# HGRN heads advanced in pairs, and the value products of a query block issued in one visit

## The chip, the cores and the metric

One NeuronCore of a Trainium2 chip runs the whole kernel. The metric is device time in microseconds of one execution; the figure used is the median of several runs.

## What is computed

Two residual layers over 512 tokens of width 1024, in float32. Each layer normalises its input, projects it to 15 pieces, runs three token mixers beside each other and merges them:

```python
for l in range(DEPTH):                       # 2
    h = rms_norm(x, norm_gain[l])
    proj = jnp.einsum('bld,dn->bln', h, w_in[l])
    (qa, fa_f, fa_b, ia, za, ub, vb, zb, qc, kc, vc, zc, g_a, g_b, g_c) = split(proj)
    # A: bidirectional gated linear recurrence, 4 heads, dk = dv = 128
    ya = rms_norm(hgrn2_bidirectional(qa, fa_f, fa_b, ia, lower[l]), hg_norm_gain[l]) * silu(za)
    # B: chunked spatial gating
    yb = spatial_gating(gelu(ub), gelu(vb), ...) * silu(zb)
    # C: windowed attention, 8 query heads on 2 kv heads, rotary, per-head sink
    yc = window_attention(q, k, vc, sink_logits[l]) * silu(zc)
    merged = sigmoid(g_a) * (ya @ w_branch_a[l]) + sigmoid(g_b) * (yb @ w_branch_b[l]) \
           + sigmoid(g_c) * (yc @ w_branch_c[l])
    x = x + merged @ w_out[l]
```

## The kernel before

**Projections.** Every weight tile of 128 x 1024 is loaded on SP's queue in the order of `weight_plan` (line 46; the host packs them in that order), split into a high part by ScalarE (line 193) and a low part by VectorE (line 194), and used in three matmuls per 128 rows of contraction: `t_block` (line 424, matmuls at line 433) with the weights stationary and 512 tokens moving, `nat_block` (line 390, matmuls at line 386) with the tokens stationary. A block of `main_t` has 24 such matmuls. `w_next` and `w_ahead` keep the loads and splits some tiles ahead.

**Side work.** The rest of the layer is written as Python generators in the list `sides`: normalisation and rotation of queries and keys, one `attention(qb)` for each of four query blocks, one `gla(h)` for each HGRN head, `ln_v` and `spatial(g)`. `advance(us)` is called in the middle and at the end of each projection block. It adds to a credit and steps the first two generators of the list (WIDTH = 2) in turn; a step yields its cost, and a yield of None makes that generator wait for the next `advance`. `flush` runs generators to their end; it stands before each of the three merge loops (lines 1010 to 1015), for attention, for the spatial part, and for everything.

**What a head does.** `gla` (line 739) builds the intra-chunk scores by levels m = 1, 2, 4, ... 128. The sum product and levels 1 to 8 are 32 products of a 32-wide stationary each, all into slots of one PSUM tile `cb` (line 769); levels 16 and 32 stand at line 794, also 32-wide, level 64 at line 803, 64-wide, level 128 at line 818, 128-wide. Between the levels VectorE copies or merges slots into `pc` (lines 782, 787, 810) and multiplies the decays into q and k (line 827) and the gates (line 830), and ScalarE mixes k for the next level (line 758). Each level ends with a cost of 2.6 and a None. Then follow a transposition (line 842), the state (line 849), the output (lines 859, 866), its normalisation, and a transposition back (line 880).

**What attention does.** For each key block of a query block VectorE transposes the probabilities in 32 x 32 pieces (line 670), POOL's queue writes them to DRAM and reads them back rearranged (lines 672, 673), four Nones later two value products of a 64-wide stationary and 512 columns follow (line 680; four instruction records for a key block).

**Order.** The program text gives each instruction a priority; within it a scheduler places, on each engine, what is ready by its own timing model, and adds all waits. Only instructions wrapped in `pin` keep their order (the loads on SP among them). In the main loop (line 948) the blocks of a head come first, then `gla(h)` joins the list; the vb projection stands behind head 0, u and z blocks of the spatial branch behind heads 1 and 2.

Of the kernel before, what the change touches and what calls it, by code (L numbers as in the profile page):

```python
# [13 lines left out]
F32 = mybir.dt.float32  # L14
# [7 lines left out]
P = 128  # L22
# [23 lines left out]
def weight_plan():  # L46

    plan = []

    def nat(c):  # L50
        for i in range(4):
            plan.append(("n", c, i))

    nat(C_QC)
    for g in range(2):
        plan.append(("z", g))
    for i in range(2):
        plan.append(("k", C_KV, i))
    for g in range(2, 4):
        plan.append(("z", g))  # L60
    nat(C_IA)
    for h in range(H):
        for c in (C_QA, C_FF, C_FB, C_ZA):
            plan.append(("t", c + P * h))
        if h == 0:
            nat(C_VB)
        elif h < 3:
            for g in (2 * h - 2, 2 * h - 1):
                plan.append(("t", C_UB + P * g))
                plan.append(("t", C_ZB + P * g))  # L70
    for br, cg in ((2, C_GC), (1, C_GB), (0, C_GA)):
        for j in range(KT):
            plan.append(("t", cg + P * j))
            if j % 2 == 0:
                plan.append(("b", br, j))
    for u in range(2):
        for i in range(4):
            plan.append(("o", u, i))
    return plan
# [51 lines left out]


N_RAW, N_HI, N_LO = 4, 5, 4
STAGGER = 2
N_M4, N_T2, N_PM, N_PS = 22, 7, 3, 5


def build(nc, tc, cp, wp, sb, pp, dp, x, wpk, brow, gainb, pvec, wsp, trig, amask, imask, out):
    V, S, G, E = nc.vector, nc.scalar, nc.gpsimd, nc.tensor
# [4 lines left out]
    def nm(s):  # L144
        cnt[0] += 1
        return f"{s}_{cnt[0]}"

    def m4(shape=(P, 1024), dt=F32):
        return sb.tile(list(shape), dt, name=nm("m4"), tag="m4", bufs=N_M4)
# [10 lines left out]
    def ps_side(shape=(P, 512), dt=F32):  # L160
        return pp.tile(list(shape), dt, name=nm("ps"), tag="ps", bufs=N_PS)
# [276 lines left out]
    sides = []  # L438
# [21 lines left out]
    def advance(us):  # L460
# [6 lines left out]
            credit[0] -= c  # L467
        credit[0] = min(credit[0], 2.0 * us if sides else 0.0)

    def flush(upto=()):  # L470
        while sides and (not upto or any(u in sides for u in upto)):
            step([])
        credit[0] = min(credit[0], 0.0)
# [3 lines left out]
    for l in range(L):  # L477
# [63 lines left out]
        vC = t2((P, NT, P))  # L541
# [77 lines left out]
        def attention(qb):  # L619
            k0, k1 = max(qb - 1, 0), min(qb + 2, NT)  # L620
            while not (("q", qb) in done and ("k", (k1 - 1) // 2) in done):
                yield None
            for _ in range(STAGGER * (qb % 2)):
                yield None
            nkb = k1 - k0
            nk = nkb * P
            off = (k0 - qb + 1) * P
            rc, dn, mxs, m, esk = small(8), small(8), small(8), small(8), small(8)
            sms, pair, pts = [], [], {}
            for h in range(8):  # L630
                g = h // 4
                if h % 2 == 0:
                    sm2 = m4((P, 2, nk))
                    pair.append(sm2)
                sms.append(sm2[:, h % 2, :])
                sp = ps_side()
                E.matmul(sp[:, :nk], qt[qb][:, h, :], ktt[0][:, g, k0 * P : k1 * P], start=True, stop=False)  # L637
                E.matmul(sp[:, :nk], qt[qb][:, h, :], ktt[1][:, g, k0 * P : k1 * P], start=False, stop=True)  # L638
                V.tensor_tensor_reduce(
                    sms[h], sp[:, :nk], am[:, off : off + nk], 1.0, NEG, ALU.add, ALU.max, mxs[:, h : h + 1]  # L640
                )
                yield 0.5
                if h == 3:
                    yield None
            V.tensor_tensor(m, mxs, sink, ALU.max)
            V.tensor_tensor(esk, sink, m, ALU.subtract)
            V.tensor_scalar_mul(m, m, -1.0)
            for h in range(8):
                S.activation(sms[h], sms[h], AF.Exp, bias=m[:, h : h + 1], accum_out=dn[:, h : h + 1])
                if h == 3:  # L650
                    yield 0.0
                    yield None
            S.activation(esk, esk, AF.Exp)
            V.tensor_tensor(dn, dn, esk, ALU.add)
            V.reciprocal(rc, dn)
            yield 0.5
            yield None
            for h in range(8):
                V.tensor_scalar_mul(sms[h], sms[h], rc[:, h : h + 1])
            yield 2.0  # L660
            yield None

            po = ps_side((P, 4, 4, 32))
            for kb in range(nkb + 1):
                if kb < nkb:
                    pt = m4((P, 4, 256))
                    xb = pt.rearrange("p b (h j) -> p b h j", j=32)
                    for i in range(4):
                        src = pair[i][:, :, kb * P : (kb + 1) * P].rearrange("p h (b j) -> p h b j", j=32)
                        V.transpose(xb[:, :, 2 * i : 2 * i + 2, :].rearrange("p b h j -> p h b j"), src)  # L670
                    pd = dp.tile([P, 4, 256], F32, name=nm("pd"))
                    G.dma_start(pd, pt)
                    G.dma_start(pt, pd.rearrange("(a j) b n -> (j b) a n", j=32))
                    pts[kb] = pt
                    yield 1.0
                for _ in range(4):
                    yield None
                if kb > 0:
                    for g in range(2):
                        E.matmul(  # L680
                            po[64 * g : 64 * g + 64],
                            vC[:, k0 + kb - 1, 64 * g : 64 * g + 64],
                            pts[kb - 1][:, :, 128 * g : 128 * g + 128],
                            start=kb == 1,
                            stop=kb == nkb,
                            tile_position=(0, 64 * g),
                        )
                    yield 1.0
            yield None
            qs = slice(qb * P, (qb + 1) * P)  # L690
            for i in range(2):
                z = szc[i][:, :, qs].rearrange("p h (a t) -> p h a t", t=32)
                V.tensor_tensor(z, po[:, :, 2 * i : 2 * i + 2, :].rearrange("p a h t -> p h a t"), z, ALU.mult)
            yield 1.5
# [11 lines left out]
        for g in range(4):  # L706
# [6 lines left out]
            po = main_t()  # L713
            z = szc[g // 2][:, g % 2, :]
# [185 lines left out]
        def ln_v():  # L900
            mv = small(8)
            mv2 = mv.rearrange("p (n c) -> p n c", c=2)
            for n in range(NT):
                st = small(6)
                V.bn_stats(st, vg[n // 2][:, n % 2, :])
                V.bn_aggr(mv2[:, n, :], st)
            r = rstd(mv2[:, :, 1], NT, 1.0)

            po = ps_side((P, 4, P))
            E.matmul(po, ones, ws, start=True, stop=True)  # L910
            for g in range(4):
                b = br[:, g * P : (g + 1) * P]
                V.scalar_tensor_tensor(b, po[:, g, :], lnb[:, g : g + 1], b, ALU.mult, ALU.add)
            yield 2.5
            yield None
            for n in range(NT):
                v = vg[n // 2][:, n % 2, :]
                V.tensor_scalar(v, v, mv2[:, n, 0:1], r[:, n : n + 1], ALU.subtract, ALU.mult)
                yield 0.7
# [24 lines left out]
            advance(2.6)  # L944


        lnv, spat = ln_v(), [spatial(g) for g in range(4)]
        for h in range(H):
            po = main_t()
            q = t2()  # L950
            S.copy(q, po)
            advance(2.6)
            ff, kd = m4((P, 2, T)), m4((P, 2, T))
            for d in range(2):
                po = main_t()
                gates(po, d, h, ff, kd)
                advance(2.6)
            po = main_t()
            z = yA[h // 2][:, h % 2, :]
            S.activation(z, po, AF.Sigmoid)  # L960
            V.scalar_tensor_tensor(z, po, hg[:, h : h + 1], z, ALU.mult, ALU.mult)
            sides.append(gla(h, q, ff, kd, z))
            advance(2.6)
            if h == 0:
                nat_units(do_vb, 2.6)
                sides.insert(0, lnv)
                if more:
                    rr = rope_row(l + 1)
                    tabs[0] = rope_tables(rr)
            elif h < 3:  # L970
                do_uz(2 * h - 2)
                do_uz(2 * h - 1)
                if h == 2:
                    sides[1:1] = spat


        acc, mgh, mgl = [], [], []
# [158 lines left out]
```

## Time and profile before

| | |
|---|---|
| median of 3 runs | 1115.63 us (1115.42 to 1116.74) |
| the profiled execution | 1115.61 us, its span 1113.8 us |
| TensorE busy | 1102.2 us (99%) in 7012 matmul records |
| weight loads busy | 895.1 us (80%) |
| VectorE busy | 699.1 us (63%) |
| ScalarE busy | 428.4 us (38%) |
| granted TensorE clock | 0.998 of full speed |

The span runs from the first to the last instruction of the program. Matmuls overlap in the records: a projection matmul is shown 0.39 us long, while the next one starts 0.23 us after it. What TensorE really spends is therefore read from the starts, or from the chain of work that ended last, which cuts the overlaps.

### The profile page before, as it was taken

Reading aid. Unit: us, or ns where it says so; the run is one execution under the profiler, and the core shown is the slowest. Engines: PE = TensorE matmul, PEld = TensorE weight load, DVE = VectorE, ACT = ScalarE, POOL = GpSimd, SP = SyncE. Lnnn points to the kernel's source line nnn. Section 1 sums busy time; section 2 is a strip of 40 time slices with the busy share of each in tenths; the row PEclk is TensorE's granted clock in tenths of the full one; section 3 lists DMA queues with packets and bytes.
Section 4 is the critical chain, followed back from the end, with each engine's and each line's share of the span. In section 5 each row is a group of like instructions: output and inputs, shape, how many; then the busy total and the mean of one; then the engine's idle time right before and its main releaser. Section 6 shows DMA issues by size and latency. Waiting matters only on the chain.

```text
span 1113.8 us, 17328 instructions
## 1 busy us (share of the span) xinstructions
PE 1102.2 (99%) x7012; PEld 895.1 (80%) x7012; DVE 699.1 (63%) x1503; ACT 428.4 (38%) x679; POOL 48.5 (4%) x71
## 2 busy tenths in 40 slices
PE   8999999999999999999999999999999999999998
PEld 6798777778878888888889887777888888888886
DVE  5966579778776533444397665987778555334432
ACT  4456355433432422232244546463434233222320
POOL 4010102000000000000000010010000000000000
PEclk9999999999999999999999999999999999999999
DMA  8242826421222233325333254562222123333431
GB/s 299 81 126 68 275 76 220 153 70 57 95 84 71 72 99 96 95 94 189 114 114 123 86 202 138 170 206 79 63 71 76 58 76 95 95 92 98 142 114 48
DMA packets 36672, 127.52 MB, mean 114 GB/s; under 512 B 4336, under 2 KB 4848, under 8 KB 36592
## 3 DMA queue, kind: packets, MB, share of 16 engines
q1 hardware_dynamic: 28656, 100.20, 28.3%
q0 software_dynamic: 6208, 22.02, 5.8%
q10 hardware_dynamic: 1728, 4.20, 1.0%
q8 instruction: 55, 0.90, 0.3%
q14 instruction: 25, 0.20, 0.1%
HBM read 111.19 MB, written 15.20 MB: 113 GB/s over the span
## 4 chain that ended last, share of the span: by engine, by line
PE 94%; DVE 3%; ACT 1%; issue 1%; DMA 0%
PE pm L433 62%; PE pm L386 19%; PE pm L421 2%; PE ps L680 2%; PE ps L769 1%; PE ps L859 1%; PE ps L638 1%; PE ps L637 1%; PE ps L818 1%; PE ps L849 1%; PE ps L924 1%; PE ps L866 1%; PE ps L794 1%; DVE m L827 0%; DVE m L810 0%
## 5 line engine op out<-in xcount | busy, mean ns | idle before, releaser
L433 PE MATMUL pm<-hth,wh 128*128 128x512 f32 x832 | 332.7, 400 | 0.0
L433 PE MATMUL pm<-htl,wh 128*128 128x512 f32 x832 | 325.0, 391 | 0.0
L433 PE MATMUL pm<-hth,wl 128*128 128x512 f32 x832 | 324.8, 390 | 0.0
L193 ACT CAST wh<-wr 128x1024 fp32r<-128x1024 f32 x172 | 180.5, 1052 | 371.2 <-PE pm L433 256.5
L194 DVE TENSOR_TENSOR wl<-wr,wh 128x1024 fp32r<-128x1024 f32 x169 | 205.5, 1219 | 177.5 <-PE pm L433 120.4
L433 PEld LDWEIGHTS pm<-hth,wh 128*128 128x128 f32 x832 | 156.2, 188 | 41.1 <-issue 8.6
L433 PEld LDWEIGHTS pm<-hth,wl 128*128 128x128 f32 x832 | 156.2, 188 | 33.3
L433 PEld LDWEIGHTS pm<-htl,wh 128*128 128x128 f32 x832 | 156.4, 188 | 30.5 <-issue 0.5
L433 PE MATMUL pm<-m,wh 128*128 128x512 f32 x384 | 119.4, 392 | 0.0
L827 DVE TENSOR_TENSOR m<-m,f 128x512 f32<-128x512 f32 x112 | 74.7, 685 | 13.6 <-PE ps L818 3.7
L433 PEld LDWEIGHTS pm<-m,wh 128*128 128x128 f32 x384 | 71.3, 188 | 14.6
L386 PE MATMUL pm<-wh,m 128*128 128x512 f32 x256 | 79.0, 389 | 0.0
L386 PE MATMUL pm<-wh,hth 128*128 128x512 f32 x192 | 74.9, 401 | 0.7 <-ACT hth L193 0.5
L386 PE MATMUL pm<-wh,htl 128*128 128x512 f32 x192 | 73.9, 395 | 1.0 <-DVE htl L194 1.0
L433 PE MATMUL pm<-m,wl 128*128 128x512 f32 x192 | 74.8, 389 | 0.0
L386 PE MATMUL pm<-wl,hth 128*128 128x512 f32 x192 | 73.7, 394 | 0.9 <-POOL wl L194 0.8
L386 PEld LDWEIGHTS pm<-wh,m 128*128 128x128 f32 x256 | 48.1, 188 | 9.9
L1000 DVE TENSOR_TENSOR t<-pm,t 128x512 f32<-128x512 f32 x32 | 22.1, 692 | 49.5 <-PE pm L433 49.5
L386 PE MATMUL pm<-wl,m 128*128 128x512 f32 x128 | 49.9, 390 | 0.0
L386 PEld LDWEIGHTS pm<-wh,hth 128*128 128x128 f32 x192 | 36.2, 189 | 12.7 <-issue 3.2
L386 PEld LDWEIGHTS pm<-wl,hth 128*128 128x128 f32 x192 | 36.2, 189 | 9.4 <-POOL wl L194 1.8
L386 PEld LDWEIGHTS pm<-wh,htl 128*128 128x128 f32 x192 | 36.4, 191 | 9.0 <-DVE htl L194 2.1
(169 smaller groups left out, 1260.8 us busy)
## 6 DMA issues: line engine op xcount, KB each, us to landing
wr<-in_wpk SPq DMA_DIRECT2D x172, 512.0 KB, 3.7
pd<-m POOLq DMA_DIRECT2D x20, 512.0 KB, 3.3
m<-pd POOLq DMA_DIRECT2D x20, 512.0 KB, 5.0
m<-in_x SPq DMA_DIRECT2D x8, 512.0 KB, 6.5
x<-m ACTq DMA_DIRECT2D x4, 512.0 KB, 2.6
m<-x SPq DMA_DIRECT2D x4, 512.0 KB, 5.8
out_dram<-m ACTq DMA_DIRECT2D x8, 256.0 KB, 2.0
m<-in_gainb SPq DMA_DIRECT2D x2, 512.0 KB, 6.3
```

The lines of the kernel that those rows point to most:

```text
L193: order(S.copy(hi_dst, src))
L194: order(eng.tensor_tensor(lo_dst, src, hi_dst.bitcast(F32), ALU.subtract))
L386: E.matmul(po, a, b[:, o : o + 512], start=first and n == 0, stop=last and n == len(passes) - 1)
L421: E.matmul(po[:, k, :], a, b[:, o : o + 256], start=n == 0, stop=n == 23)
L433: E.matmul(po, s, m, start=n == 0, stop=n == 3 * nk - 1)
L637: E.matmul(sp[:, :nk], qt[qb][:, h, :], ktt[0][:, g, k0 * P : k1 * P], start=True, stop=False)
L638: E.matmul(sp[:, :nk], qt[qb][:, h, :], ktt[1][:, g, k0 * P : k1 * P], start=False, stop=True)
L680: E.matmul(po[64 * g : 64 * g + 64], vC[:, k0 + kb - 1, 64 * g : 64 * g + 64], pts[kb - 1][:, :, 128 * g : 128 * g + 128], start=kb == 1, ...
L769: E.matmul(cb[p0 : p0 + 32, slot, j // 4, :], kk(32 * j), qq(32 * j), start=True, stop=True, tile_position=(0, p0),)
L794: E.matmul(dg[p0 : p0 + 32, j // 4, f0 : f0 + 32], kx[:, 32 * j : 32 * j + 32] if m == 16 else k_op(32 * j, m), q_op(32 * jq, m), start=Tr ...
L827: V.tensor_tensor(v, v, custom(ff, of, ([sd, 2], [2, ng], [0, m])), ALU.mult)
L1000: V.tensor_tensor(sg, po, sg, ALU.mult)
```

## The change

Heads 0 and 1, then heads 2 and 3, are wrapped by a new generator `together`: one visit runs a step of the first head and the same step of the second, and yields the sum of their costs. A pair joins the list when both heads are projected. The vb projection moves from behind head 0 to behind head 1, and with it the rope row and tables of the next layer; the u and z blocks move from behind heads 1 and 2 to behind heads 1 and 3; the spatial generators follow head 3. `weight_plan` follows that order. In `attention` all key blocks are transposed and sent first, one per step at a cost of 1.7 instead of 1.0; after six empty steps (LAG) all value products of the query block are issued together.

```diff
--- before.py
+++ after.py
@@ -62,10 +62,10 @@
     for h in range(H):
         for c in (C_QA, C_FF, C_FB, C_ZA):
             plan.append(("t", c + P * h))
-        if h == 0:
+        if h == 1:
             nat(C_VB)
-        elif h < 3:
-            for g in (2 * h - 2, 2 * h - 1):
+        if h % 2 == 1:
+            for g in (h - 1, h):
                 plan.append(("t", C_UB + P * g))
                 plan.append(("t", C_ZB + P * g))
     for br, cg in ((2, C_GC), (1, C_GB), (0, C_GA)):
@@ -131,7 +131,7 @@
 
 
 N_RAW, N_HI, N_LO = 4, 5, 4
-STAGGER = 2
+STAGGER, LAG = 2, 6
 N_M4, N_T2, N_PM, N_PS = 22, 7, 3, 5
 
 
@@ -466,6 +466,22 @@
                 break
             credit[0] -= c
         credit[0] = min(credit[0], 2.0 * us if sides else 0.0)
+
+    def together(gens):
+
+        gens = list(gens)
+        while gens:
+            cost = 0.0
+            for g in list(gens):
+                c = 0.0
+                while c is not None:
+                    cost += c
+                    c = next(g, "end")
+                    if c == "end":
+                        gens.remove(g)
+                        c = None
+            yield cost
+            yield None
 
     def flush(upto=()):
         while sides and (not upto or any(u in sides for u in upto)):
@@ -660,32 +676,32 @@
             yield 2.0
             yield None
 
+            for kb in range(nkb):
+                pt = m4((P, 4, 256))
+                xb = pt.rearrange("p b (h j) -> p b h j", j=32)
+                for i in range(4):
+                    src = pair[i][:, :, kb * P : (kb + 1) * P].rearrange("p h (b j) -> p h b j", j=32)
+                    V.transpose(xb[:, :, 2 * i : 2 * i + 2, :].rearrange("p b h j -> p h b j"), src)
+                pd = dp.tile([P, 4, 256], F32, name=nm("pd"))
+                G.dma_start(pd, pt)
+                G.dma_start(pt, pd.rearrange("(a j) b n -> (j b) a n", j=32))
+                pts[kb] = pt
+                yield 1.7
+                yield None
+            for _ in range(LAG):
+                yield None
             po = ps_side((P, 4, 4, 32))
-            for kb in range(nkb + 1):
-                if kb < nkb:
-                    pt = m4((P, 4, 256))
-                    xb = pt.rearrange("p b (h j) -> p b h j", j=32)
-                    for i in range(4):
-                        src = pair[i][:, :, kb * P : (kb + 1) * P].rearrange("p h (b j) -> p h b j", j=32)
-                        V.transpose(xb[:, :, 2 * i : 2 * i + 2, :].rearrange("p b h j -> p h b j"), src)
-                    pd = dp.tile([P, 4, 256], F32, name=nm("pd"))
-                    G.dma_start(pd, pt)
-                    G.dma_start(pt, pd.rearrange("(a j) b n -> (j b) a n", j=32))
-                    pts[kb] = pt
-                    yield 1.0
-                for _ in range(4):
-                    yield None
-                if kb > 0:
-                    for g in range(2):
-                        E.matmul(
-                            po[64 * g : 64 * g + 64],
-                            vC[:, k0 + kb - 1, 64 * g : 64 * g + 64],
-                            pts[kb - 1][:, :, 128 * g : 128 * g + 128],
-                            start=kb == 1,
-                            stop=kb == nkb,
-                            tile_position=(0, 64 * g),
-                        )
-                    yield 1.0
+            for kb in range(nkb):
+                for g in range(2):
+                    E.matmul(
+                        po[64 * g : 64 * g + 64],
+                        vC[:, k0 + kb, 64 * g : 64 * g + 64],
+                        pts[kb][:, :, 128 * g : 128 * g + 128],
+                        start=kb == 0,
+                        stop=kb == nkb - 1,
+                        tile_position=(0, 64 * g),
+                    )
+            yield 1.0
             yield None
             qs = slice(qb * P, (qb + 1) * P)
             for i in range(2):
@@ -944,6 +960,7 @@
             advance(2.6)
 
 
+        glas = []
         lnv, spat = ln_v(), [spatial(g) for g in range(4)]
         for h in range(H):
             po = main_t()
@@ -959,19 +976,21 @@
             z = yA[h // 2][:, h % 2, :]
             S.activation(z, po, AF.Sigmoid)
             V.scalar_tensor_tensor(z, po, hg[:, h : h + 1], z, ALU.mult, ALU.mult)
-            sides.append(gla(h, q, ff, kd, z))
+            glas.append(gla(h, q, ff, kd, z))
+            if h % 2 == 1:
+                sides.append(together(glas[-2:]))
             advance(2.6)
-            if h == 0:
+            if h == 1:
                 nat_units(do_vb, 2.6)
-                sides.insert(0, lnv)
+                sides.insert(1, lnv)
                 if more:
                     rr = rope_row(l + 1)
                     tabs[0] = rope_tables(rr)
-            elif h < 3:
-                do_uz(2 * h - 2)
-                do_uz(2 * h - 1)
-                if h == 2:
-                    sides[1:1] = spat
+            if h % 2 == 1:
+                do_uz(h - 1)
+                do_uz(h)
+            if h == 3:
+                sides[1:1] = spat
 
 
         acc, mgh, mgl = [], [], []
```

## Rows read from the trace of the kernel before

**Rows 1.** The page: busy time of two engines, and the granted clock by slices.
```profile
PE 1102.2 (99%) x7012; PEld 895.1 (80%) x7012; DVE 699.1 (63%) x1503; ACT 428.4 (38%) x679; POOL 48.5 (4%) x71
...
PEclk9999999999999999999999999999999999999999
```

**Rows 2.** The chain of work that ended last: start us, us, what.
```profile
188.99 1.01 PE ps L680 x4
189.99 11.11 PE pm L433 x48
...
216.14 0.39 PE ps L769 x32
216.53 2.94 PE pm L433 x12
...
377.76 141.49 PE pm L433 x624
...
673.81 1.87 PE ps L680 x8
```

**Rows 3.** Waits of TensorE and SP: who <- whom: us, times, longest us.
```profile
PE ps L818 <- DVE m L827: 0.7, 3, 0.4
PE ps L769 <- DVE pc L782: 0.6, 2, 0.3
...
SPq L257 <- DVE sm L646: 17.5, 1, 17.5
```

**Rows 4.** The chain again, 300 to 332 us, where two heads shared a step.
```profile
311.22 0.69 PE ps L769 x50
...
330.98 0.62 PE ps L803 x16
331.60 0.39 PE ps L769 x32
```

**Rows 5.** TensorE's timeline, 233 to 242 us: start us, us, instruction [idle before <-releaser].
```profile
233.76 0.46 PE L769 MATMUL ps<-t,t 128*32 128x32 f32 x32
234.15 0.50 PE L433 MATMUL pm<-hth,wh 128*128 128x512 f32 x1
...
237.45 0.39 PE L433 MATMUL pm<-hth,wl 128*128 128x512 f32 x1
238.12 0.54 PE L769 MATMUL ps<-m,t 128*32 128x32 f32 x32 [0.28 <-DVE pc L782]
...
240.54 0.39 PE L433 MATMUL pm<-hth,wl 128*128 128x512 f32 x1
240.76 1.05 PE L818 MATMUL ps<-m,m 128*128 128x128 f32 x8
```

**Rows 6.** VectorE, 207 to 377 us by line (last: busy, mean ns), and its timeline.
```profile
L827 DVE TENSOR_TENSOR m<-m,f 128x512 f32<-128x512 f32 x55 | 36.8, 685 | 7.9 <-PE ps L818 2.3 <-PE ps L794 2.3 <-PE ps L803 1.6
L194 DVE TENSOR_TENSOR wl<-wr,wh 128x1024 fp32r<-128x1024 f32 x22 | 26.9, 1222 | 21.3 <-PE pm L433 21.3
L830 DVE TENSOR_TENSOR f<-f 128x128 f32<-128x128 f32 (+5 forms) x22 | 4.7, 222 | 0.1
L787 DVE COPY_PREDICATED pc<-im,ps 128x128 f32<-128x128 int32 x16 | 4.7, 296 | 1.7 <-PE ps L769 1.7
...
320.65 0.69 DVE L827 TENSOR_TENSOR m<-m,f 128x512 f32<-128x512 f32 x1
...
328.82 0.69 DVE L827 TENSOR_TENSOR m<-m,f 128x512 f32<-128x512 f32 x1
```

**Rows 7.** DMA issues (KB, us to landing), and POOL's timeline of three transfers.
```profile
pd<-m POOLq DMA_DIRECT2D x20, 512.0 KB, 3.3
m<-pd POOLq DMA_DIRECT2D x20, 512.0 KB, 5.0
...
655.42 0.55 POOL L672 DMA_DIRECT2D pd<-m  x1 [11.05 <-DVE m L670]
...
667.17 0.77 POOL L673 DMA_DIRECT2D m<-pd  x1 [5.22 <-issue]
```

## Prediction

> **What bounds the kernel now.** I read the page first: TensorE is busy 99% of the span, VectorE 63%, and the clock is at full speed in every slice [rows 1]. A busy matmul engine need not be at its peak, so next I read the chain of work that ended last. It is TensorE almost throughout, and its long stretches give the pitch: 624 projection matmuls run undisturbed in 141.49 us, 0.2267 us each [rows 2]. The list of waits leaves TensorE only 1.3 us of idle time on VectorE in the recurrence (0.7 and 0.6 us) [rows 3]. So time goes only where TensorE issues something dearer, and I took the small products one by one.
>
> **The price of a visit.** Between two stretches of projection matmuls stands one group of 32 tiny products (128x32 stationary, 32 columns, line 769). The chain gives it 0.39 us, and the 12 matmuls behind it take 2.94 us instead of 12 x 0.2267 = 2.72 us [rows 2]. One lone group costs 0.39 + 0.22 = 0.61 us. Where two groups of 32-wide products of two heads stand together, at 311.22 us, both take 0.69 us [rows 4]: the second costs 0.69 - 0.39 = 0.30 us. A join of two 32-wide groups is therefore worth 0.31 us. Where a 32-wide group follows a 64-wide one (0.62 then 0.39 us, at 330.98 us) the second costs 0.39 us and the join is worth 0.61 - 0.39 = 0.22 us [rows 4]. The value products (line 680, 64-wide, 512 columns): a lone group is 1.01 us, and the 48 matmuls behind it take 11.11 us for 48 x 0.2267 = 10.88 us, so it costs 1.01 + 0.23 = 1.24 us; two together take 1.87 us, the second 0.86 us, a join is worth 0.38 us [rows 2]. Groups with a full 128-wide stationary show no such price at their start: line 818 begins 0.22 us behind the last projection matmul, the ordinary pitch [rows 5]. So joins count only among lines 769, 794, 803 and 680.
>
> The Trainium skill, page "TensorEngine Tiling (Array Packing)", section Performance Considerations, speaks against the change: each matmul is said to carry some 60 cycles of overhead, whatever its columns. By that the price would lie in the instructions, whose number is unchanged, and joining would save nothing: the time would stay 1115.6 us. The second group of 32 products took 0.30 us, 9 ns a product, half of what the lone group cost, so the trace does not bear that out here. The same page, section Tiling Modes, Key Properties, says that a change of tiling mode drains the engine, which is in line with the price per change of width.
>
> **Part 1, heads in pairs.** A head has eight such groups: the sum product and levels 1, 2, 4, 8 (line 769), levels 16 and 32 (line 794), level 64 (line 803). Two layers with two pairs each give 4 x 8 = 32 possible joins. I take all at 0.31 us; that of two line-803 groups shows nowhere in the trace, and lies between the 0.22 and the 0.38 us of its neighbours [rows 2, 4]. Not all will come out. Instructions are placed by readiness, not only in the order written: level 1 of a head must wait until VectorE has copied the sum product out of the same bank (line 782), and at 233.76 us 15 projection matmuls slipped in between (234.15 to 237.45 us), after which TensorE still sat 0.28 us [rows 5]. So of each pair's joins I drop the one at level 1. I drop one more, where VectorE is late for the second head: a level costs it two multiplications (0.685 each), one predicated copy (0.296) and a gate product (0.222), 1.89 us for a head and 3.8 us for both [rows 6]. That leaves 6 x 4 = 24 joins, 24 x 0.31 = 7.4 us; bounds 0 (none) and 32 x 0.31 = 9.9 us, and with the sum and level-1 products of both heads in one stretch 4 x 0.31 = 1.2 us more. I lean to the upper end, since the nearest rows, at 311 to 331 us, are two heads visited in one step, and all three pairs of groups stood together [rows 4].
>
> **Part 2, value products.** 20 groups (80 instructions of line 680, four to a group) become one visit for each of 8 query blocks: 12 joins x 0.38 = 4.6 us. Their operands go to DRAM and back over POOL's queue: write issue, a wait for its landing, read issue. One trip takes 3.3 us to the landing of the write and 5.0 us to that of the read, 8.3 us; three at once take from 655.42 us (first write) to 667.17 us (last read) plus 5.0 us, about 17 us [rows 7]. The new code writes three blocks in three successive steps of about 2.8 us and waits six steps: the last transfer has 7 x 2.8 = 20 us. With two blocks in flight five or six trips share that time; at 17/3 = 5.7 us each the sixth lands some 34 us after the first write, against 6 + 20 = 26 us plus the lag of the second block. Late data here lets projection matmuls go first, and costs then a lost join (0.38 us), not a stall; if the placement took the transfer for quicker than it is, TensorE would stand up to 8 us, but no wait of TensorE for these transfers shows now [rows 3], with the shorter lag. I take the 4.6 us whole, with the waits as the nearest row; the ends are 4.6 us gained and 8 us lost, and the loss goes with rival B.
>
> **Part 3, what is given up.** The present order has joins by chance, read off TensorE's timeline: one of line 680 with itself (0.38), three of 32-wide groups (311.2, 318.3 and 324.6 us, 0.93, of which the first stands in the rows), seven of 32-wide with 64-wide groups (207.7, 222.7, 233.1, 331.0, 754.4, 768.7, 814.1 us, 7 x 0.22 = 1.54) [rows 2, 4]. The 12 and 32 joins are counted from a kernel with none, so these 2.9 us come off.
>
> **Part 4, what moves.** The vb projection goes behind head 1, the u and z blocks behind heads 1 and 3. The number of projection matmuls is the same; their weights go through the packed order, and SP's loads keep their sequence. The rope row and its two table loads now go onto SP's queue behind head 1: today SP stands 17.5 us there for the last sink use (line 646), with the weight loads behind it, and no wait of TensorE for weights follows [rows 3]. The row comes 8 blocks later, attention ends earlier, so I cost it at nothing; the weights already loaded are the cover, now as before. Counting the yields, attention needs 13 to 14 steps a block for up to 21, so pair 0 finds a free slot during vb, no later than head 0 does now, which also waits until attention leaves a slot. A pair visit costs 5.2 of credit, paid by two steps of 2.6: one per 24 matmuls. The second pair starts after head 3 and ends within the first merge loop; today layer 0's last small product ends where the undisturbed stretch begins, at 377.76 us [rows 2]. The only flush that waits for heads stands before the third merge loop; a loop is 8 x 36 matmuls, 65.3 us, so it begins 65.3 us before the end of the stretch (377.76 + 141.49 = 519.25 us), at 454 us. There are 76 us to spare, so nothing spills. If some did, each level would cost what it costs now plus VectorE's 1.9 us, some 8 us for half a pair's levels.
>
> **New waits.** Both heads now ask for VectorE at once, with weight splits (1.22 us) between. When two heads shared a step, VectorE was done with them 3.2 us and 1.4 us before the next visit: 320.65 + 0.69 against 324.6, 328.82 + 0.69 against 330.98 [rows 4, 6]. That is little. A pair visit behind a u block needs 3.8 + 1.22 + 1.8 us (gelu: two multiplications and a scaling, an estimate from the 0.685 us) = 6.8 us of VectorE in 24 x 0.2267 + 0.9 = 6.3 us. Behind a waiting product on TensorE's queue stand the projection matmuls, and behind those everything. Today's waits are 1.3 us; bounds -1.3 us (all gone) and 36 pair visits (nine with products, four pairs) x 0.28 us (the wait at 238.12 us) = 10 us [rows 5]. I take +1.0 us, near today's sum, since most late products are passed by rather than waited for.
>
> **Sum.** The profiled execution took 1115.61 us (span 1113.8 us and 1.8 us around it), the median 1115.63 us: no correction. 1115.6 - 7.4 - 4.6 + 2.9 + 1.0 = **1107.5 us**.
>
> **Rivals.**
> A. The heads do not stand together: placement by readiness separates them as it separates line 769 from itself at 233 us, and only the value products join. 1115.6 - 4.6 + 2.9 + 1.0 = 1114.9 us, within 0.2%. Against it: the three joined visits of layer 0. Chance 0.16.
> B. Slower: VectorE becomes the limit of each pair visit. The second head's operands come 1.9 us later than now; 36 visits that each wait t. It decides at t = (7.4 + 4.6 - 2.9 + 2.2) / 36 = 0.31 us. With the 6.8 - 6.3 = 0.5 us that a visit behind a u block lacks, at every visit, 18 us, and the time would be 1115.6 - 9.1 + 18 = 1124.5 us. For it speaks the 6.8 us of work in 6.3 us; against it that VectorE is busy 63% of the span [rows 1], that blocks without gelu leave it more room, and that late products are passed by. Chance 0.13.
> C. Everything joins and no wait comes: 1115.6 - 9.9 - 1.2 - 4.6 + 2.9 = 1102.8 us. Chance 0.09.
> The forecast, 1104 to 1113.3 us, has 0.62.
>
> **Chances.** About 0.2% (2.2 us) is what a measurement of this kernel can tell from no change. Faster: 0.62 + 0.09 and a small part of A, 0.72. Same: 0.15. Slower: 0.13. The range 1103.5 to 1114.0 us takes in the forecast with the bounds of its joins and waits, and leaves out B, most of A and the best end of C.
>
> **What would show it.** TensorE's timeline: line 769 in runs of 64 (0.69 us) instead of 32, line 680 in runs of 8 or 12; 40 to 50 stretches of narrow products where 73 stand now (counted on the timeline). The waits for VectorE (lines 782 and 827) tell of B: above 5 us in all, it has begun. The prediction is wrong if line 769 still stands in 32s, if TensorE shows idle time before lines 769 or 680, or if the last small product comes behind the second merge loop.

## Result and the profile after

The change makes the kernel faster: 1103.96 us (1103.14 to 1105.53, four runs) against 1116.18 us for the kernel before, measured beside it; ratio 0.9892, 95% interval 0.9875 to 0.9909. The forecast was 1107.5 us: right in sign and inside its range, but a third too small in size. It came out close to rival C.

The page of the changed kernel, against [rows 1]: TensorE is still 99% busy, in 12 us less.

```profile
span 1101.3 us, 17346 instructions
...
PE 1090.9 (99%) x7012; PEld 897.7 (82%) x7012; DVE 699.6 (64%) x1503; ACT 427.3 (39%) x679; POOL 48.8 (4%) x71
```

The chain of work that ended last (start us, us, what), against [rows 2, 4]. The line numbers have moved: 785 was 769, 810 was 794, 819 was 803, 696 was 680, 834 was 818. The chain cuts overlapping records, so of 64 records it may show 50.

```profile
166.55 2.73 PE ps L696 x12
...
175.86 0.69 PE ps L785 x50
176.99 0.86 PE ps L785 x64
...
186.96 1.87 PE ps L696 x8
...
204.54 0.69 PE ps L785 x50
205.23 5.69 PE pm L433 x24
...
226.40 1.08 PE ps L819 x32
...
233.15 1.78 PE ps L834 x16
234.93 5.46 PE pm L433 x24
...
372.35 141.49 PE pm L433 x624
```

Every group of line 785 stands in a run of 64: 0.69 us for two heads, as the pair at 311.22 us in [rows 4], and 0.82 to 0.86 us at level 1, which follows the sums after one to three projection matmuls. Behind most of these runs 24 projection matmuls stand undisturbed, where 12 did. Value products come in runs of 8 and 12: 1.01, 1.87 and 2.73 us for one, two and three key blocks, 0.86 us for each further one. The undisturbed stretch of 624 matmuls takes 141.49 us again, so nothing came from the projections themselves; it begins 5.4 us earlier, and the second layer saves the rest.

The list of waits of TensorE (who <- whom: us in total, times, longest), against [rows 3]. Lines 316, 240 and 386 belong to the start of the kernel.

```profile
PE ps L316 <- DVE m L306: 1.9, 2, 1.7
PE ps L240 <- POOL ident masks.py:199: 1.3, 1, 1.3
PE pm L386 <- DVE htl L194: 1.0, 1, 1.0
PE pm L386 <- POOL wl L194: 0.9, 1, 0.9
PE pm L386 <- ACT hth L193: 0.7, 3, 0.3
PE ps L653 <- DVE sm L655: 0.4, 1, 0.4
```

Lines 782 and 827, with 0.6 and 0.7 us before, are gone from it. SP's wait of 17.5 us for the sink is gone from SP's list as well, without a gain to be seen on TensorE.

One correction to the words of the prediction and of the description of the kernel before: a group of 32 records of line 769 or 794 is 16 products of two records each, so 0.30 us are 19 ns a product, 9 ns a record. Every sum above goes by groups and stands.

### The profile page after: what moved, and what is told of

It reads as the page before. It is cut to its first block, busy times and chain, and to the rows that moved or that the text cites. A ratio compares the mean times of both kernels' runs of the same rounds, so it can differ in the third digit from the quotient of the medians.

```text
span 1101.3 us, 17346 instructions
## 1 busy us (share of the span) xinstructions
PE 1090.9 (99%) x7012; PEld 897.7 (82%) x7012; DVE 699.6 (64%) x1503; ACT 427.3 (39%) x679; POOL 48.8 (4%) x71
## 4 chain that ended last, share of the span: by engine, by line
PE 96%; DVE 2%; ACT 1%; DMA 1%; issue 0%; POOL 0%; POOLq 0%; ACTq 0%
PE pm L433 63%; PE pm L386 19%; PE pm L421 2%; PE ps L696 1%; PE ps L785 1%; PE ps L875 1%; PE ps L653 1%; PE ps L654 1%; PE ps L240 1%; DMA wr<-in_wpk 1%; PE ps L834 1%; PE ps L865 1%; PE ps L882 1%; PE ps L940 1%; PE ps L316 1%; PE ps L810 1%
## 5 line engine op out<-in xcount | busy, mean ns | idle before, releaser
L433 PEld LDWEIGHTS pm<-hth,wh 128*128 128x128 f32 x832 | 156.2, 188 | 35.1 <-issue 2.9
L433 PEld LDWEIGHTS pm<-hth,wl 128*128 128x128 f32 x832 | 156.2, 188 | 33.3 <-DVE wl L194 0.2
```

Source lines behind the costliest of these rows:

```text
L433: E.matmul(po, s, m, start=n == 0, stop=n == 3 * nk - 1)
```

## Experiments

Theory J says that the time is the number of joins times their price. Theory O says that the gain comes from what moved (vb and u, z blocks, the rope row, the earlier end of attention). The table collects all runs; each is told below. Joins are counted in the order of TensorE's instructions, 32-wide with 32-wide / 64-wide with 64-wide (level 64 and value products) / mixed. "Visits" are places after 48 us where other products stand between projection matmuls. "Beyond" is worked out from the starts on TensorE's timeline after 48 us: all time beyond 0.2272 us a projection matmul (0.113 us for those of 256 columns). It leaves out the first 48 us, in which the profiles differ by up to 1.6 us (112 to 119 matmuls done by then).

Two groups count as joined also where a few projection matmuls cut one of them in the middle. Each run was measured beside the kernel before, which took 1116.2 to 1116.6 us; the ratios below are to that.

| kernel | median us | joins | visits | beyond us |
|---|---|---|---|---|
| before | 1116.2 | 3 / 1 / 7 | 124 | 150.7 |
| the change | 1104.0 | 28 / 16 / 1 | 100 | 137.5 |
| e1_heads | 1111.9 | 25 / 6 / 2 | 111 | 145.5 |
| e2_values | 1117.3 | 0 / 12 / 3 | 136 | 151.2 |
| e3_apart | 1113.2 | 0 / 12 / 2 | 148 | 148.4 |
| e4_break | 1111.5 | 8 / 16 / 1 | 104 | 145.5 |
| e5_nobreak | 1106.1 | 24 / 16 / 1 | 104 | 139.9 |
| e8_sum | 1101.9 | 32 / 16 / 1 | 96 | 135.7 |
| e6_lag2 | 1122.5 | 29 / 8 / 0 | 114 | 156.2 |
| e6b_lag4 | 1105.0 | 27 / 16 / 1 | 101 | 138.8 |
| e7b_dve2 | 1106.6 | 26 / 16 / 1 | 104 | 142.2 |
| e7_dve5 | 1129.6 | 12 / 12 / 1 | 124 | 164.6 |
| e9_rope | 1117.1 | 0 / 12 / 3 | 136 | 151.5 |
| e11_early | 1105.0 | 27 / 16 / 1 | 103 | 139.7 |

**Is it the joins or the order?** The whole change with one head to a visit:

```diff
-            cost = 0.0
             for g in list(gens):
-                c = 0.0
+                cost, c = 0.0, 0.0
                 while c is not None: ...
-            yield cost
-            yield None
+                yield cost
+                yield None
```

> The whole change, but a visit steps one head of the pair only, the other head in the next visit; order of blocks, attention and costs as in the change. Theory J: no join of 32-wide groups is left, 12 of value products and 2 mixed remain, 4.6 + 0.4 = 5.0 us against 2.9 us before: 2.2 us less than before, about 1114.0 us. Theory O: the order is the change's, so the gain stays: about 1104 us.

Measured: 1113.21 us, ratio 0.9972 (0.9961 to 0.9983). Three quarters of the gain are gone with the joins of the heads: 9.2 us for 32 joins (28 and 4 of level 64), 0.29 us each. What is left, the order with the value visits, keeps 3 us, near the 2.2 us that theory J gives to the value visits. Theory O, which asked for 1104 us, falls. Its chain (784 is line 769 of before, 809 is 794, 818 is 803) shows lone groups in the rhythm of [rows 2], 0.39 us and 2.94 us for 12 matmuls:

```profile
211.91 0.39 PE ps L784 x32
212.30 2.94 PE pm L433 x12
215.24 0.39 PE ps L809 x32
215.63 2.94 PE pm L433 x12
...
228.58 0.62 PE ps L818 x16
229.20 2.94 PE pm L433 x12
```

The last two lines give a price that the prediction had to bound: a lone group of level 64 costs 0.62 + 0.22 = 0.84 us, two take 1.08 us (line 819 above), so the second costs 0.46 us and the join is worth 0.38 us.

**Is it the change of width?** The change with one small product between the two heads' groups of line 785, once with a full stationary and once with a 32-wide one:

```diff
             def compact(slot, kk, qq):
+                if h % 2 == 1:
+                    pin(E.matmul(cb[:, slot, 0, :], ident, ident[:, :32], start=True, stop=True))
                 for j in range(16):
```

> The change with one product more, of a full 128-wide stationary and 32 columns, ahead of each line-769 group (sum, levels 1, 2, 4, 8) of the second head: 20 in all. It separates the two heads' groups by a change of width and nothing else. Theory J: 20 joins are lost (8 of 28 remain), 20 x 0.31 = 6.2 us, and 20 products of some 0.05 us: about 1104.0 + 7.2 = 1111 us. Theory O: 20 small products cost 1 us: 1105 us.

> The same 20 extra products with a 32-wide stationary, so that no width changes. Theory J: 4 joins are lost, since the pinned product puts level 1 of one head ahead of the sum of the other, 1.2 us, and 20 x 0.02 us: about 1105.6 us, some 5 us below the kernel with the 128-wide products. Theory O: the same as with the 128-wide ones.

(In the second the output is `cb[0:32, slot, 0, :]`, the stationary `ident[:, :32]`, with `tile_position=(0, 0)`.) Measured: 1111.48 us, ratio 0.9957 (0.9943 to 0.9970), and 1106.07 us, ratio 0.9907 (0.9894 to 0.9921). As many instructions, 5.4 us apart, for 16 joins: 0.34 us each. Some of it is the guest's own work: reckoned from the starts, a parted visit costs 1.33 us where two lone groups cost 2 x 0.61 = 1.22 us, so the full-width guest takes some 0.1 us itself. The first fence is the chain with the full stationary, the second that with the 32-wide one; line 787 are the narrow groups, 784 is the guest:

```profile
205.65 0.39 PE ps L787 x32
206.04 0.34 PE ps L784 x2
206.37 0.39 PE ps L787 x32
206.76 5.67 PE pm L433 x24
```

```profile
204.29 0.39 PE ps L787 x32
204.68 0.01 PE ps L784
204.69 0.34 PE ps L787 x23
205.03 5.67 PE pm L433 x24
```

1.11 us against 0.74 us for the same 32 products and one guest. So the price goes with the change of width and not with the number of instructions; e3, without a guest, gives about the same for a join. Another rival is that these products are of another kind than the projections (two records each, a projection matmul has one). Against it stand products of two records with a full-width stationary: 16 records of line 834 take 1.78 us, 0.11 us each, and the 24 matmuls behind them 5.46 us, for 24 x 0.2267 = 5.44 us (233.15 us on the chain of the change). The Trainium skill, page "TensorEngine Tiling (Array Packing)", section Tiling Modes, Key Properties, agrees: changing the tiling mode, not just the tile, drains the engine. It gives no price; here it is 0.31 to 0.38 us for leaving the full width and coming back.

**The parts alone.** e1 puts the old attention loop into the change, e2 puts the new loop into the kernel before.

> Heads in pairs and blocks moved as in the change; attention as before, one visit for each key block. Theory J (the time is the number of joins between narrow groups times their price, 0.31 us for 32-wide with 32-wide and for line 803 with itself, 0.38 us for value products, 0.22 us for mixed widths). Its instruction order has 25 joins of 32-wide groups, 4 of level 64, 2 of value products and 2 mixed: 7.8 + 1.2 + 0.8 + 0.4 = 10.2 us against 2.9 us of the kernel before, so 7.3 us less: about 1108.8 us. Theory O (the gain comes from the moved blocks and the earlier end of attention, not from the joins): the blocks are moved here too but attention keeps its length, so part of 12 us, anything from 1104 to 1116 us.

> Attention alone as in the change (all value products of a query block in one visit); heads and blocks as before. Theory J: 12 joins of value products and 3 mixed, 4.6 + 0.7 = 5.2 us against 2.9 us that the chance joins of the kernel before were worth, so 2.4 us less: about 1113.8 us. Theory O: attention ends earlier and heads start earlier, as in the change, so most of the 12 us: about 1106 us.

Measured: 1111.92 us, ratio 0.9962 (0.9949 to 0.9974), and 1117.33 us, ratio 1.0010 (1.0001 to 1.0018). Both miss theory J by 3 us and more, and the two gains add up to 3.6 us where the whole has 12.2. Neither theory foresaw that. Most of the difference can be found on the timelines. Reckoned from the starts, with the prices above and 0.11 us for a full-width record, the narrow visits take 4.2 us more in e1 and 3.1 us more in e2 than their groups and joins are worth; it is 0.9 us in the change and 0.6 us in the kernel before. In e1 the four value records of one key block stand two and two, at 199.5 and 203.9 us, the first pair with 1.3 us of delay, and there are six delays of 0.4 to 0.5 us, most of them where groups were parted. In e2 there are 1.6 us at 179.4 us, where two of a visit's eight value records come late and alone, and two delays of 0.4 us:

```profile
179.37 1.07 PE L680 MATMUL ps<-m,t 128*64 128x512 f32 x2 [0.49 <-DMA m<-pd]
180.98 0.50 PE L433 MATMUL pm<-hth,wl 128*128 128x512 f32 x1 [0.54 <-DVE wl L194]
```

Just then POOL worked on the next layer's rope tables between two transfers (its timeline; 671 issues a read back, 265 and 268 are the tables):

```profile
171.41 0.77 POOL L671 DMA_DIRECT2D m<-pd  x1
173.94 0.57 POOL L265 TENSOR_SCALAR rr<-rr 128x128 f32<-128x128 f32 x1 [1.75 <-DMA rr<-in_brow]
175.28 1.18 POOL L268 TENSOR_TENSOR tabs<-tabs,rr 128x256 f32<-128x256 f32 x1 [0.77 <-DMA tabs<-in_trig]
176.81 0.82 POOL L671 DMA_DIRECT2D m<-pd  x1 [0.35 <-DMA pd<-m]
```

The rows themselves speak against the tables as the cause. The read that TensorE waited for was issued at 171.41 us, ahead of them, and landed at 179.32 us, 7.9 us later, where the median of the kernel before is 5.0 us [rows 7]; the next read waited for the landing of its own write. What made the read slow is not shown.

Theory R, that the tables are why attention alone gained nothing, was tried from both sides: e9 is e2 with the row behind head 1, e11 the change with the row behind head 0.

```diff
+            if h == 1 and more:          # e9; in e11: h == 0
+                rr = rope_row(l + 1)
+                tabs[0] = rope_tables(rr)
```

> Attention alone as in the change, heads as in the kernel before, and the next layer's rope row and tables (SP loads, POOL multiplications) moved from behind head 0 to behind head 1. Theory R (attention alone brought nothing because POOL's tables stood between the value transfers and TensorE waited 1.6 us for one, at 179 us): the wait goes, about 1.6 us less than with the row behind head 0, 1115.5 us. Rival V (the price is the larger number of visits, 136 for 124, and lost chance joins): no difference, 1117 us.

> The change with the rope row and tables put back behind head 0, everything else the change's. Theory R: the value transfers of query blocks 2 and 3 meet POOL's tables again, a wait of 1 to 2 us in layer 0, and three joins of 32-wide groups fewer by its instruction order (27 for 28, and 42 stretches for 39), 1 us: about 1106 us. Rival: the move costs nothing either way, 1104.5 us.

Measured: 1117.05 us, ratio 1.0008 (0.9999 to 1.0017), and 1104.95 us, ratio 0.9898 (0.9884 to 0.9911). In e9 that wait is gone, though the visit is still parted, and another came, at 211.6 us, for VectorE's copy (from its list of waits):

```profile
PE ps L769 <- DVE pc L782: 1.6, 1, 1.6
```

Theory R falls as the reason for the time; rival V's number is met, yet V itself is not shown. In e11 a value visit of layer 0 stands in two parts, with 0.4 us of delay at each, and the time is 1 us above the change's, about the scatter of either (1104.4 to 1105.9 and 1103.1 to 1105.5 us): costing the rope row's move at nothing was about right. What stays open is why the parts alone run into such waits and parted groups and the whole does not; in both parts attention and heads overlap otherwise than in the change.

**The copy of the sum.** Level 1 can be written before the sum is copied out:

```diff
-            V.tensor_copy(pc, cb[:, 0])
             while m < 256:
                 if m <= 8:
                     ...
+                    if m == 1:
+                        V.tensor_copy(pc, cb[:, 0])
```

> The change, and VectorE copies the sum product out of the bank only after the level-1 products are written, so that both groups of both heads can stand together. Theory J: 4 more joins of 0.31 us, 1.2 us less than the change: about 1102.7 us. Rival: the copy comes later, level 2 is late on VectorE and TensorE waits: 1104 us or more.

Measured: 1101.94 us, ratio 0.9871 (0.9858 to 0.9885): the fastest of all, 2.0 us below the change, with 4 joins more and 4 visits fewer. Theory J gives the joins 1.2 us; where the rest comes from is not shown, and the profiled executions differ by 1.5 us. Both groups of both heads stand together (a run of 128 records):

```profile
176.18 1.42 PE ps L785 x123
177.60 5.66 PE pm L386 x24
```

1.42 us, against 0.69 and 0.86 us with projection matmuls between.

**How much cover the transfers have.** LAG 2 and 4 instead of 6 (one constant).

> The change with 2 empty steps instead of 6 between the last transfer of a query block and its value products: 3 steps of 2.8 us = 8.4 us for a round trip of 8.3 us alone. If placement by readiness covers a late transfer with projection matmuls, the price is lost joins: 8 joins of 64-wide groups remain instead of 16, 29 of 32-wide, so about 2.7 us more, 1106.5 us, and TensorE doesn't wait for transfers. Rival: TensorE waits for them up to 8 us for each of 8 query blocks: 1110 us or more.

> The change with 4 empty steps instead of 6: 5 steps of 2.8 us, 14 us for the last transfer of a query block. Where the cover of the transfers ends between 3 and 7 steps: if 14 us are enough, as the one-trip time of 8.3 us and 17 us for three at once suggest for the later blocks, about 1104.5 us; if the blocks that go together in layer 0 need more, waits of 1 to 6 us and the lower clock behind them, 1106 to 1112 us.

Measured: 1122.51 us, ratio 1.0058 (1.0044 to 1.0071), and 1105.01 us, ratio 0.9905 (0.9890 to 0.9920). With 2 steps the rival's mechanism holds: TensorE waits, late transfers are not all passed by, and the time is 12 us above the rival's lower bound. Its waits, its timeline and its granted clock (columns: stretch, us, busy us and instructions of PE, PEld, DVE, ACT, POOL, granted clock, DMA share, GB/s):

```profile
PE ps L696 <- DMA m<-pd: 12.3, 7, 5.6
```

```profile
126.53 2.28 PE L696 MATMUL ps<-m,t 128*64 128x512 f32 x8
134.45 1.98 PE L696 MATMUL ps<-m,t 128*64 128x512 f32 x4 [5.64 <-DMA m<-pd]
136.36 0.79 PE L433 MATMUL pm<-hth,wh 128*128 128x512 f32 x1
136.95 0.63 PE L433 MATMUL pm<-htl,wh 128*128 128x512 f32 x1
137.38 0.63 PE L433 MATMUL pm<-hth,wl 128*128 128x512 f32 x1
```

```profile
120.00:126.00 6.00, 6.00 (x30) 5.16 (x29) 5.41 (x13) 2.55 (x3) 0.77 (x1) 1.00 0.91 279
126.00:134.00 8.00, 2.69 (x11) 0.57 (x9) 2.18 (x4) 7.32 (x20) 0.77 (x1) 0.96 0.89 313
134.00:141.00 7.00, 6.55 (x16) 4.00 (x17) 4.45 (x15) 1.44 (x2) 0.00 (x0) 0.55 0.00 1
```

After a 5.64 us wait the clock stands near its lower level, 1.2 GHz (0.55 in the stretch), and the matmuls start 0.43 us apart instead of 0.23. With 4 steps only 1.1 us of such waits are left, and the time (1104.1 to 1107.8 us) can't be told from the change's. The change's own 6 steps leave little in one place: the last of the transfers that go together in layer 0 lands at 133.9 us (20.6 us after the first of its three writes at 113.3), the products start at 135.3 us.

**How much cover VectorE has.** More multiplications of 128x256 (measured 0.424 us each) ahead of line 843's, 5 or 2 for each level and head:

```diff
+                for _ in range(5):
+                    V.tensor_tensor(junk, kd[:, 0, :256], kd[:, 1, :256], ALU.mult)
                 for t, of, sd in ((qd, 1, nb - 1), (kd, nb + 1, -nb - 1)):
```

> The change with five more VectorE multiplications of 128x256 (estimate 0.42 us each) in each level of each head, ahead of those that the next level needs: 4.2 us more of VectorE in each pair visit. Where the late product is passed by, the price is lost joins: 12 of 28 of 32-wide groups and none of level 64 remain, 20 x 0.31 = 6.2 us: about 1110 us with hardly a wait on TensorE. Rival B (VectorE becomes the limit): waits of TensorE before lines 769 to 803, 32 visits of up to 3 us: 1120 us or more.

> The change with two more VectorE multiplications of 128x256 in each level of each head instead of five: about 1.7 us more in each pair visit. If the slack of VectorE in a pair visit is about 1.4 us as the rows of the kernel before suggest, waits begin here: 1106 to 1109 us. If it is larger, only 2 lost joins and small ones: 1105 us. Waits as large as with five: 1112 us or more.

Measured: 1129.64 us, ratio 1.0121 (1.0107 to 1.0135), and 1106.61 us, ratio 0.9914 (0.9901 to 0.9928). 4.2 us more of VectorE in a pair visit make rival B real. 1.7 us more cost 2.6 us of time, and one narrow visit waits (its list of waits; 811 is line 810 of the change):

```profile
PE ps L811 <- ACT t L775: 1.2, 1, 1.2
```

So VectorE had less than 1.7 us to spare there, some 0.5 us by 1.7 - 1.2 (an estimate), while 26 of the 28 joins of 32-wide groups still came. Waits and timeline of the run with five (its lines stand one to three behind those of the change; 775 is ScalarE's mix of k):

```profile
PE ps L811 <- ACT t L775: 4.1, 2, 3.3
PE pm L434 <- DVE wl L194: 3.9, 3, 1.9
...
PE ps L835 <- DVE m L846: 1.5, 3, 0.8
```

```profile
765.12 0.66 PE L811 MATMUL ps<-m,t 128*32 128x32 f32 x32 [3.27 <-ACT t L775]
765.88 0.80 PE L434 MATMUL pm<-hth,wl 128*128 128x512 f32 x1
766.48 0.63 PE L434 MATMUL pm<-hth,wh 128*128 128x512 f32 x1
766.90 0.63 PE L434 MATMUL pm<-htl,wh 128*128 128x512 f32 x1
```

TensorE waits not only for products of the heads but for weight splits (line 194) that VectorE does late, and again the matmuls behind run 0.43 us apart.

## Why the prediction was right, and where its size was off

- **The price of a visit** (0.31 us for a join) held: e3 gives 9.2 / 32 = 0.29 us, and e4 against e5 5.4 / 16 = 0.34 us, with the extra products in it. By the 60 cycles a matmul of the Trainium skill's page "TensorEngine Tiling (Array Packing)", section Performance Considerations, e4 and e5 would have been equal; the runs disagree.
- **Part 1** was the most mis-sized term, by 2.8 us. I took 24 of 32 joins, 7.4 us; all 32 came, 28 at 0.31 us and 4 of level 64 at 0.38 us, 10.2 us. The step that failed is the loss at level 1: from one head parted from its own sum in [rows 5] I concluded that two heads' level 1 would part from each other. They are parted from their sums together (0.69 us, one to three projection matmuls, 0.82 to 0.86 us) and stand in a run of 64. The second loss, VectorE late for the second head, didn't come either.
- **Part 2**: 12 joins, 4.6 us, as taken. The reckoning of six trips at 5.7 us was too dark: the last landed 1.4 us ahead of its product. The caution was in place, as LAG 2 shows.
- **Part 3**: 2.9 us given up, and one mixed join (0.2 us) came anew at 727.1 us, where a value visit touches line 785.
- **Part 4**: nothing, as costed; the last small product of layer 0 ends at 372.35 us, far ahead of the third merge loop.
- **New waits** were taken at +1.0 us. They went the other way: from 1.3 us to 0.4 us, -0.9 us. This term was 1.9 us too dark. The 6.8 us of VectorE work in 6.3 us was counted for the worst block and did not hold the visits up; by e7b most visits have 1.7 us to spare, and one some 0.5 us.

With the measured terms: -10.2 - 4.6 - 0.2 + 2.9 - 0.9 = -13.0 us; the profiled span fell by 1113.8 - 1101.3 = 12.5 us, the medians by 12.2 us. Rival A fell with the runs of 64, B by the waits. C, at a chance of 0.09, was nearest (1102.8 us), though the 1.2 us that it added for sum and level 1 came only with e8.

That the time fell inside the stated range was in part luck. 1103.96 us lies 0.46 us above the range's lower end and just below the 1104 to 1113.3 us that had a chance of 0.62; and the kernel before, measured beside it, took 1116.18 us, 0.6 us more than the 1115.6 us from which the forecast was reckoned. From 1115.6 us the same gain of 12.2 us would have ended at 1103.4 us, outside.

## What to carry to other kernels

Where one engine is busy throughout, count how often it changes between kinds of work (here between widths of the stationary), and price one change from two rows of the trace: a lone group and a joined one. Joining works as long as the operands of both partners are ready at one time, so measure the cover on the engine and the transfers that feed them; below it, the waits can cost more than all joins bring, as in e6 and e7. And two parts of such a change need not add up: here each alone fell into waits that the whole avoids.

## What the runs showed of the hardware

I had not expected the second price of a long wait: behind 5.64 us and behind 3.27 us of idle TensorE the projection matmuls ran 0.43 us apart, with a granted clock of 0.55 in the seven microseconds around the first, against 1.00 before it. From the value products at 134.45 us to the return of the usual pitch at 140.33 us passed 5.88 us, for work that takes 1.01 + 0.22 + 9 x 0.2267 = 3.27 us at full speed, so the wait cost 2.6 us more; behind the wait of 3.27 us it was 1.9 us by the same reckoning (765.12 to 769.46 us). And the 64-wide groups of level 64, joined with their like, save more (0.38 us) than the 32-wide ones (0.31 us).
